# Where TensorE's operand tiles begin in SBUF: 32 bytes past a multiple of 64, or on it

## The chip, the cores and the metric

The kernel runs on one core of a Trainium2 chip. The metric is the device time of one execution in microseconds; of the kernel before there are three runs. A profiled execution of its own gives the trace, whose times count from the first instruction.

## The reference

One layer of a two-branch attention trunk is computed in fp32, for a prompt of 1024 tokens and for 64 sample tokens that carry a cache of 512 keys. The model width is 1024.

```python
h = rms_norm(x, w) @ w_in                       # 1024 -> 6144 columns
sb_q, sb_k, sb_v, sb_z, cb_q, cb_k, cb_v, cb_z, g_sb, g_cb = split(h)
# branch A, stick-breaking: 8 heads x 64
z = q . k * 0.125
log_keep = where(causal, log_sigmoid(-z), 0)
w = where(causal, exp(log_sigmoid(z) + suffix_sum(log_keep)), 0);  o_sb = w @ v
# branch B, chunk band: 8 heads x 64, softmax over at most 576 keys, relative bias
o_cb = softmax(qn . kn * 0.125 + bias) @ v
b_sb = (o_sb * silu(sb_z)) @ w_proj_sb;  b_cb = (o_cb * silu(cb_z)) @ w_proj_cb
y = x + (sigmoid(g_sb) * b_sb + sigmoid(g_cb) * b_cb) @ w_out
```

The new keys and values of both branches are outputs as well.

## The kernel before

T is 1088 columns: 1024 prompt tokens and 64 sample tokens. Every large product is made of three matmuls in the type fp32r. Each operand is split into a high part (a copy rounded to fp32r, on ScalarE) and a low part (the remainder, on GpSimd or VectorE), and high x high, low x high and high x low are summed in PSUM. So each matmul of these products has its own weight load of 128 columns (LDWEIGHTS, "PEld" in the profile), and then streams 256 to 512 columns of the other operand, the moving one. Only the transposes (`ident` is the moving operand) and the product with the values (L1115) are plain fp32.

The program is written out in one order for each engine; no scheduler moves anything. Its stages, as TensorE goes through them:

- **L464**, the projection to values and to the keys and queries of branch B, tokens on the output's partitions: 8 blocks of 256 columns of `w_in`, 9 groups of tokens each. The moving operand is the weights (`whi`, `wlo`, `whix`, `wlox`, 256 columns), the stationary one the normed tokens `xa`, `xm`, `xb` (or `xs` for the sample tokens). That is 8 x (16 + 8 x 24) = 1664 matmuls. Between groups stand transposes at L277, L349 and L371.
- **L634**, the projection to branch A's keys and queries and to the silu gates, by a Strassen-like scheme of seven products: 8 x 7 x 2 x 12 = 1344 matmuls, half of 256 and half of 288 columns. The tokens (`xa`, `xm`, `xb` and their sums `t0h` to `t3l`) move, the weights are stationary.
- **Attention** of both branches, 8 pairs of heads, while L773 fills TensorE with the gates' projections (16 units x 72 = 1152 matmuls, two thirds of 384 and one third of 320 columns). L1024 and L1025 are q.k (224 matmuls each, together 153,600 columns); L1076 transposes the attention weights, L1115 multiplies with the values. Branch A has on VectorE a scan along the keys (L1044) in the tile `kp`, which has three buffers used in turn. L873 (288 matmuls, as wide as L773's) is branch A's projection.
- **L917**, branch B's projection: 192 matmuls of 384 and 96 of 320 columns.
- **L1409** and L1445, the output projection, again by seven products: 672 and 64 matmuls of 256 columns.

The tiles lie in pools. The pools on the left are stacked upwards from `consts`, the pools on the right downwards from the end of SBUF; `xpool` is the first on the right, and holds `xa`, `xm` and `xb`. A tile's address follows from what was opened before it, so a `pad`, a tile that nothing uses, moves all that is stacked behind it:

```python
consts = ctx.enter_context(tc.tile_pool(name="consts", bufs=1))
def pad(pool, n):
    pool.tile([128, n // 4], F32, name=f"pad{n}", bufs=1)
pad(consts, 96)
ident = consts.tile([128, 128], F32, name="ident")
make_identity(nc, ident)
pad(consts, 64)
wpool = ctx.enter_context(tc.tile_pool(name="wp", bufs=2))
...
xpool = ctx.enter_context(tc.tile_pool(name="xn", bufs=1, side="right"))
```

Other pads of 64 bytes stand at the heads of the pools `tp`, `ak`, `am` and `hp`. With all of them, in each matmul but 112 transposes one operand begins 32 bytes and the other 96 bytes past a multiple of 128; in those 112 both begin 96 past. So every operand of TensorE, all 7128 matmuls over, begins 32 bytes past a multiple of 64. Rows inside the tiles keep this, since their lengths and the steps between slices are multiples of 64 bytes.

Of the kernel before, what the change touches and what calls it, by code (L numbers as in the profile page):

```python
# [32 lines left out]
def hybrid_step_kernel(ctx: ExitStack, tc: tile.TileContext, x_prompt, x_sample, c_sbk, c_sbv, c_cbk, c_cbv,  # L33
# [54 lines left out]
    consts = ctx.enter_context(tc.tile_pool(name="consts", bufs=1))  # L88

    def pad(pool, n):  # L90
        pool.tile([128, n // 4], F32, name=f"pad{n}", bufs=1)

    pad(consts, 96)
    ident = consts.tile([128, 128], F32, name="ident")
    make_identity(nc, ident)
    pad(consts, 64)
# [38 lines left out]
    xpool = ctx.enter_context(tc.tile_pool(name="xn", bufs=1, side="right"))  # L135
    x0 = xpool.tile([128, 4, T], F32R, name="xa")
    xm = xpool.tile([128, 2, 4, T], F32R, name="xm")
    x3 = xpool.tile([128, 4, T], F32R, name="xb")
    xhl = [[x0[:], xm[:, 0]], [xm[:, 1], x3[:]]]

    def xk(s, k):
# [1353 lines left out]
```

## Time and profile before

| | |
|---|---|
| median of 3 runs | 1000.83 us (999.85 to 1001.19) |
| profiled execution, span | 1000.1 us, 20177 instructions |
| TensorE: matmul / weight load | 977.8 us (98%) / 930.8 us (93%), 7512 each |
| VectorE / ScalarE / GpSimd | 657.0 us (66%) / 472.9 us (47%) / 324.9 us (32%) |
| granted TensorE clock, mean | 0.998 |
| DMA | 169.83 MB, mean 170 GB/s |

How to read it: the busy time of a matmul counts its way through the array, so that neighbours overlap; what one costs in a stream is the distance from its start to the next one's start. The chain of work gives that distance at once: a row such as "2.73 PE acc L464 x24" is 24 matmuls in 2.73 us with no wait between them. L1115's matmuls stand as two records each, which is why the profile has 7512 and the program 7128.

### The profile page before, as it was taken

To read this page: it belongs to the slowest core of one execution; us is meant where nothing else is said; L and a number is where in the kernel's file an instruction comes from. 1 tells how busy PE (TensorE), PEld (TensorE's weight loads), DVE (VectorE), ACT (ScalarE), POOL (GpSimd) and SP (SyncE) were. 2 spreads that over 40 slices of the span, in tenths; PEclk is the share of its full clock that TensorE was granted. 3 is DMA by queue.
4 is the path that set the end of the run, shared out by engine and by line. 5 is a ranking of instruction groups with operands and counts; after the bars stand their busy time and mean duration, and the time that the engine had idled before them with its cause. 6 is when DMAs were issued, how large, how long until landed. Compare 5 with 4: busy or idle time off the path is not lost.

```text
span 1000.1 us, 20177 instructions
## 1 busy us (share of the span) xinstructions
PE 977.8 (98%) x7512; PEld 930.8 (93%) x7512; DVE 657.0 (66%) x1233; ACT 472.9 (47%) x1075; POOL 324.9 (32%) x338
## 2 busy tenths in 40 slices
PE   5999999999999999999999999999999899999998
PEld 5999999999999999988898888898989798999998
DVE  5456674895455454099898878565766766499735
ACT  5534443444344433277676656454445434365320
POOL 3276663215445543211111101110202200386552
PEclk9999999999999999999999999999999999999999
DMA  7726577424656332786566544765656854773642
GB/s 237 224 92 221 189 249 256 150 91 150 198 155 192 102 97 85 188 228 187 146 166 159 160 114 117 206 200 152 193 150 186 253 168 147 242 224 101 196 136 89
DMA packets 180865, 169.83 MB, mean 170 GB/s; under 512 B 34912, under 2 KB 167136, under 8 KB 180640
## 3 DMA queue, kind: packets, MB, share of 16 engines
q1 hardware_dynamic: 172048, 160.23, 54.2%
q10 hardware_dynamic: 8720, 8.33, 2.6%
q8 instruction: 59, 0.97, 0.4%
q14 instruction: 38, 0.31, 0.1%
HBM read 109.78 MB, written 58.72 MB: 168 GB/s over the span
## 4 chain that ended last, share of the span: by engine, by line
PE 92%; DMA 2%; DVE 2%; ACT 1%; SPq 1%; issue 1%; POOL 1%; DVEq 0%; ACTq 0%
PE acc L464 19%; PE acc L773 18%; PE b L634 17%; PE b L1409 8%; PE o L1115 7%; PE pt L1076 6%; PE b L917 5%; PE z L1025 3%; PE z L1024 3%; PE acc L873 3%; PE pk L349 1%; DMA wrawx<-in_w_in_dram 1%; DMA gt<-d_gsb 1%; DVE be L1045 1%; PE pt L277 1%
## 5 line engine op out<-in xcount | busy, mean ns | idle before, releaser
L122 POOL TENSOR_TENSOR wlo<-wraw,whi 128x1024 fp32r<-128x1024 f32 x30 | 74.2, 2473 | 243.9 <-ACT whi L115 209.2
L773 PE MATMUL acc<-xm,whi 128*128 128x384 f32 (+1 forms) x384 | 128.5, 335 | 0.0
L1044 DVE TENSOR_TENSOR_SCAN kp<-kp,imp 64x576 f32<-64x576 f32 (+8 forms) x72 | 102.8, 1427 | 21.3 <-ACT kp L1027 21.1
L1034 ACT ACTIVATE be<-be,sm 128x640 f32<-128x640 f32 (+5 forms) x72 | 50.8, 705 | 97.1 <-DVE sm L1030 97.1
L1076 PE MATMUL pt<-ident,be 128*128 128x128 f32 (+2 forms) x608 | 90.1, 272 | 6.4 <-DVE wT L1087 3.4
L1085 ACT ACTIVATE wT<-pt 128x512 f32<-128x512 f32 (+3 forms) x130 | 63.6, 502 | 55.1 <-PE pt L1076 55.1
L1076 PEld LDWEIGHTS pt<-ident,be 128*128 128x128 f32 (+2 forms) x608 | 68.5, 140 | 18.4 <-issue 6.4
L464 PE MATMUL acc<-whi,xa 128*128 128x256 f32 x256 | 74.2, 292 | 0.0
L773 PEld LDWEIGHTS acc<-xm,whi 128*128 128x128 f32 x384 | 72.5, 189 | 1.1
L464 PE MATMUL acc<-wlox,xm 128*128 128x256 f32 x256 | 70.8, 278 | 0.0
L464 PE MATMUL acc<-whi,xm 128*128 128x256 f32 x256 | 70.8, 278 | 0.0
L464 PE MATMUL acc<-wlo,xa 128*128 128x256 f32 x256 | 70.7, 278 | 0.0
L464 PE MATMUL acc<-whix,xb 128*128 128x256 f32 x256 | 70.7, 278 | 0.0
L464 PE MATMUL acc<-whix,xm 128*128 128x256 f32 x256 | 70.6, 278 | 0.0
L1115 PE MATMUL o<-wT,vp 128*64 128x256 f32 (+1 forms) x608 | 66.7, 359 | 0.0
L1045 DVE TENSOR_TENSOR be<-be,kp 64x576 f32<-64x576 f32 (+8 forms) x72 | 60.3, 837 | 9.6
L1027 ACT ACTIVATE kp<-z 128x384 f32<-128x384 f32 (+6 forms) x112 | 54.3, 485 | 24.4 <-PE z L1025 22.9
L773 PE MATMUL acc<-xa,wlo 128*128 128x384 f32 (+1 forms) x192 | 65.4, 341 | 0.0
L773 PE MATMUL acc<-xa,whi 128*128 128x384 f32 (+1 forms) x192 | 65.3, 340 | 0.0
L773 PE MATMUL acc<-xm,wlo 128*128 128x384 f32 (+1 forms) x192 | 65.1, 339 | 0.0
L1115 PEld LDWEIGHTS o<-wT,vp 128*64 128x64 f32 x608 | 42.5, 137 | 23.7 <-issue 7.6
L773 PE MATMUL acc<-xb,whi 128*128 128x384 f32 (+1 forms) x192 | 64.0, 333 | 0.0
(298 smaller groups left out, 3017.2 us busy)
## 6 DMA issues: line engine op xcount, KB each, us to landing
wraw<-in_w_in_dram SPq DMA_DIRECT2D x35, 512.0 KB, 4.7
wrawx<-in_w_in_dram SPq DMA_DIRECT2D x13, 512.0 KB, 4.4
sq<-d_qsbT SPq DMA_DIRECT2D x32, 192.0 KB, 4.7
sq<-d_qcbT SPq DMA_DIRECT2D x32, 192.0 KB, 3.7
gt<-d_gsb SPq DMA_DIRECT2D x30, 192.0 KB, 2.7
xt<-in_x_prompt_dram SPq DMA_DIRECT2D x8, 512.0 KB, 5.1
d_kcbT<-hl SPq DMA_DIRECT2D x8, 512.0 KB, 4.5
d_qcbT<-hl SPq DMA_DIRECT2D x8, 512.0 KB, 5.6
```

The costliest lines, as they stand in the source:

```text
L122: (eng or G).tensor_tensor(out=l, in0=raw, in1=h[:].bitcast(F32), op=OP.subtract)
L464: TE.matmul(ps, x, w, start=m == 0, stop=m == len(steps) - 1)
L634: TE.matmul(ps[:, :m], w[:, hl_, k], right[s](x)[:, k, a:b], start=s < 3 and k == 0 and e == 0, stop=k == 3 and e == 2, skip_group_check=s ...
L773: TE.matmul(ps[:, :b - a], w[:, k], xk(x, k)[:, a:b], start=k == 0 and n == 0, stop=k == KT - 1 and n == 2)
L1027: A.activation(kp[:r, x:y], z[:r, :m], AF.Sigmoid, scale=-0.125)
L1034: A.activation(be[:r, :n], be[:r, :n], AF.Exp, bias=kp[:r, j:j + 1], scale=-1.0, accum_out=kp[:r, 2:3])
L1044: V.tensor_tensor_scan(kp[:r, n - 1::-1], kp[:r, n - 1::-1], im[:, ::-1], 0.0, op0=OP.mult, op1=OP.add)
L1045: V.tensor_tensor(out=be[:r, :n], in0=be[:r, :n], in1=kp[:r, 1:n + 1], op=OP.mult)
L1076: TE.transpose(pt[:kr, x, :r], be[:r, kb * 128:kb * 128 + kr], ident[:r, :r])
L1085: A.activation(w[:, sl:sl + m, q0:q0 + r], pt[:, :m, :r], AF.Copy)
L1115: TE.matmul(o[hd * 64:hd * 64 + 64, c0:c1], vv[:kr, kb, hd * 64:hd * 64 + 64], wT[b, p, j, hd, s // 4][:kr, s % 4, c0:c1], start=si == 0, ...
L1409: TE.matmul(ps[:, t], left[s](xs_, k)[:, ts_], wt_[:, k], start=s < 3 and t == k == e == 0, stop=k == 3 and e == 2, skip_group_check=s > 2 ...
```

## The change

One pad grows by 32 bytes, and `xpool` gets a pad of 96 bytes at its tail, which lies below it on the right:

```diff
-    pad(consts, 96)
+    pad(consts, 128)
     ident = consts.tile([128, 128], F32, name="ident")
...
     x3 = xpool.tile([128, 4, T], F32R, name="xb")
+    pad(xpool, 96)
     xhl = [[x0[:], xm[:, 0]], [xm[:, 1], x3[:]]]
```

All tiles on the left move up by 32 bytes, all on the right down by 96. In the built program:

| tile | first byte before (past a multiple of 128) | after |
|---|---|---|
| `ident` | 1248 (96) | 1280 (0) |
| `whi`, first buffer | 10016 (32) | 10048 (64) |
| `xa` | 159712 (96) | 159616 (0) |
| `xs` | 151520 (96) | 151424 (0) |
| `t0h` | 46944 (96) | 46976 (0) |
| `ks`, first buffer | 31072 (96) | 31104 (0) |
| `sq0` | 69536 (32) | 69568 (64) |
| `be`, first buffer | 89504 (32) | 89536 (64) |
| `og0` | 112480 (96) | 112512 (0) |
| `kp`, its three buffers | 124512 (96), 128640 (0), 132768 (32) | 124544 (0), 128672 (32), 132800 (64) |

Modulo 128 everything moves by the same 32 bytes, so that the two operands of a matmul stay 64 bytes apart; modulo 256 the tiles on the right move by 128 bytes against those on the left. Instructions, their order on each engine, their semaphores and their shapes are the same in both programs; nothing but addresses differs. Line numbers behind the added line grow by one.

## The prediction

> **What bounds the kernel now.** I read the page first, then the table of what TensorE waited for, then the chain of waits for the distance between matmuls.
>
> ```profile
> span 1000.1 us, 20177 instructions
> PE 977.8 (98%) x7512; PEld 930.8 (93%) x7512; DVE 657.0 (66%) x1233; ACT 472.9 (47%) x1075; POOL 324.9 (32%) x338
> PEclk9999999999999999999999999999999999999999
> PE 92%; DMA 2%; DVE 2%; ACT 1%; SPq 1%; issue 1%; POOL 1%; DVEq 0%; ACTq 0%
> ```
>
> ```profile
> PE pt L277 <- DVE xn L266: 8.1, 2, 7.4
> PE pt L1076 <- DVE wT L1087: 3.4, 3, 2.4
> PE pt L1076 <- ACT wT L1085: 2.4, 3, 1.3
> PE acc L464 <- ACT whi L115: 2.1, 1, 2.1
> ...
> ```
>
> TensorE is busy for 98% of the span at full granted clock, it makes up 92% of the chain that ended last, and it waited 8.1 us for its first input and a few microseconds altogether after that. The kernel is a stream of matmuls; its time is their number times the distance from one to the next. So a change that alters nothing but addresses matters through that distance, or hardly at all. Here it is, in pieces of the chain without a wait in them (start, length, line, count):
>
> ```profile
> 21.00 0.87 PE pt L277 x8
> 121.04 2.73 PE acc L464 x24
> 124.42 2.84 PE acc L464 x24
> 256.11 30.02 PE b L634 x240
> 865.45 47.37 PE b L917 x288
> 925.53 16.32 PE b L1409 x144
> ```
>
> L464 with 256 columns: 2.73 / 24 = 113.8 ns in one group and 2.84 / 24 = 118.3 ns in the next, with the same code and shapes. L1409, also 256 columns: 16.32 / 144 = 113.3 ns, always. L634, half 256 and half 288 columns (272 on average): 125.1 ns. L917, two thirds 384 and one third 320 (362.7): 164.5 ns. Per column these are 0.443 ns (L1409), 0.460 (L634) and 0.454 (L917). The cost goes with the columns, and it has two levels.
>
> The transposes give the row beside it: a plain fp32 matmul of 128 columns takes 0.87 / 8 = 108.75 ns. If fp32 takes two beats for a column where fp32r takes one (the reading under which a beat, 0.425 ns, comes near the fp32r rates), 256 fp32r columns should cost 108.75 ns too. They cost 113.3 at best. That is 4% more in the quickest stream of the kernel, and 8 to 9% more in the slower ones. For the widest stream, three starts in a row in the timeline:
>
> ```profile
> 700.06 0.40 PE L1024 MATMUL z<-ks,sq 128*128 128x512 f32 x1
> 700.29 0.40 PE L1025 MATMUL z<-ks,sq 128*128 128x512 f32 x1
> 700.53 0.33 PE L773 MATMUL acc<-xm,whi 128*128 128x384 f32 x1
> ```
>
> 235 ns for 512 columns, 0.459 each: twice 113.3 and a little. An excess that doubles with the columns is not a price per instruction; something is paid again and again along the moving operand. Each operand begins 32 bytes past a multiple of 64. If TensorE fetches 64 bytes (16 fp32 columns) at a time, counted from the operand's start, every second fetch straddles a multiple of 128. That is the reason for my forecast. No row shows a straddle, because all operands of before lie alike.
>
> **The change part by part.** Nothing is removed, added or reordered, and no wait changes. Three kinds of access move.
>
> *VectorE, ScalarE, GpSimd.* Before has a natural trial: `kp`'s three buffers take turns, and of each pair of scans below the first uses the buffer that begins on a multiple of 64, the second one that begins 32 past it.
>
> ```profile
> 430.12 0.68 DVE L1044 TENSOR_TENSOR_SCAN kp<-kp,imp 128x256 f32<-128x256 f32 x1
> 431.41 0.68 DVE L1044 TENSOR_TENSOR_SCAN kp<-kp,imp 128x256 f32<-128x256 f32 x1
> 442.99 1.48 DVE L1044 TENSOR_TENSOR_SCAN kp<-kp,imp 128x640 f32<-128x640 f32 x1
> 445.34 1.48 DVE L1044 TENSOR_TENSOR_SCAN kp<-kp,imp 128x640 f32<-128x640 f32 x1
> ```
>
> No difference: 0. The rows of ScalarE and GpSimd hold no such pair; I take 0 for them as well, and TensorE's work covers them: were each 1% slower, that would be 4.7 and 3.2 us spread over the whole span, beside a busy TensorE.
>
> *DMA.* The SBUF ends of all transfers move by 32 or 96 bytes. They are on the path at the start, where this transfer ends last, and a few times later (2% of the chain):
>
> ```profile
> 2.95 7.94 DMA wrawx<-in_w_in_dram
> ```
>
> A tenth of it either way would be 0.8 us; I take 0.
>
> *TensorE.* The sum, at 0.425 ns a column as the clean price, from the transposes:
>
> - L464: between 113.8 and 118.3 I take 116.0; clean 256 x 0.425 = 108.8; 7.2 ns x 1664 = 12.0 us.
> - L634: 125.1 against 115.6; 9.5 x 1344 = 12.8 us.
> - L917 and L873: 164.5 against 154.1; 10.4 x 576 = 6.0 us.
> - L773, the same widths: 10.4 x 1152 = 12.0 us.
> - L1024 and L1025: 153,600 columns x 0.0285 (L917's excess per column) = 4.4 us.
> - L1409 and L1445: 113.3 against 108.8; 4.5 x 736 = 3.3 us.
> - Transposes, L1115: 0. They already run at the clean price.
>
> 50.5 us in all. Bounds for the unknown: above, all of it; below nothing, if every stream fell to the slow level of L464, 118.3 / 256 = 0.462 ns a column. The streams hold 1.76 million columns, which cost today 193 (L464) + 168 (L634) + 284 (L773, L873, L917) + 83 (L1409, L1445) + 70 (L1024, L1025) = 798 us; at 0.462 they would cost 813, so 15 us more.
>
> The Trainium skill (TensorE: Matmul & The Clock Gate, Back-to-back issue gap) gives for a stream of bf16 matmuls at full clock the columns over 2.4 GHz plus about 2.5 ns. That would be 109.2 ns for 256 columns, where this trace has 113.3 to 118.3 in fp32r; by that rule all the excess can go, and the sum would be an estimate of 50 us as well.
>
> What of it reaches the end: L464, L634, L873, L917, L1409 and L1445 are 34.1 us in stages where the chain is TensorE's nearly without a break. In attention, 16.4 us, the others are closer:
>
> ```profile
> 390.00:640.00 250.00, 246.03 (x1749) 221.81 (x1747) 187.31 (x228) 152.99 (x368) 35.46 (x88) 0.99 0.62 163
> 640.00:850.00 210.00, 206.22 (x1499) 186.61 (x1500) 138.74 (x442) 97.32 (x234) 29.88 (x27) 1.00 0.64 181
> ```
>
> ```profile
> 619.76 2.21 DVE kp L1044
> 622.09 1.24 DVE be L1045
> 627.90 3.11 DMA d_gcb<-sg
> 631.58 0.95 ACT whi L115
> ```
>
> VectorE (the third busy time) is at 187 of 250 us there, and around 620 us the chain already leaves TensorE for it. What is late next when TensorE quickens is the long scans; I let two thirds of the 16.4 through, 11. So 34 + 11 = 45 us. The profiled execution spans 1000.1 us and the median is 1000.8; from the latter, 1000.8 - 45 = 955.8, and I say 956.
>
> **The rivals.**
>
> *Only the slow level goes.* The step per column, 0.443 in L1409, may be the port's own rate for 4-byte columns, and only what is above it a matter of where the weight load and the moving operand meet. For: L1409 stands at 113.3 throughout, as if it could not go lower, and begins 32 past a multiple of 64 as L464 does, which jumps between 113.8 and 118.3; so the two levels do not come from the alignment alone. Then 1.76 million columns at 0.443 are 779 us, 19 less, of which 17 come through by the same shares: 984.
>
> *The change does nothing to time.* If the hardware's unit is 32 bytes or smaller, both programs are alike: all operands move by the same 32 bytes modulo 128. For: the scans' rows. Against: VectorE reads a scan of 640 elements in 1.48 us, 2.3 ns an element, a fifth of the rate of TensorE's stream; so what it hides, TensorE need not. 1000.8. The Trainium skill (SBUF — State Buffer, Specifications) speaks of 16-byte cachelines; 32 is a multiple of 16, and by that rule nothing moves. No run here shows a line's size.
>
> *Slower: the streams lock.* The next weight load reads SBUF while the present matmul streams. Today each fetch lies across two 64-byte halves; on a multiple of 64 it lies in one, and two readers that meet in the same half wait for each other every time instead of by half. The two levels of L464 show that some meeting of this kind exists and that it stays for a whole group of 24. Besides, tiles on the right move by 128 bytes modulo 256 against those on the left, which can swap quick groups for slow ones. Place: L464, L634, L773, L917, L1409. Price: all at 0.462, +15 us, 1016, since a slower TensorE is on the path everywhere. It decides once L1409 and more than half of L464's groups stand at 118.
>
> **How the numbers follow.** The straddle goes: 0.36, 956. Only the slow level goes: 0.2, 984. Nothing: 0.17, 1000.8. Slower: 0.27, 1016 and less. The step that goes with the columns speaks for the first, and that VectorE sees nothing against it; for a mere shift by 32 bytes I see fewer ways to lose than to gain. The range reaches from the whole 50.5 us and the rounding of the rows (0.01 us in 24 matmuls, 2.5 us over all 5,920 fp32r matmuls), 948, to 1016; the first case alone would be 948 to 966. About 0.2% is what a measurement of this kernel can tell from no change. Faster by more than that: 0.56; within it: 0.17; slower: 0.27.
>
> **What would show it.** Right: L1409's pieces of 144 at 15.7 us or less instead of 16.32, L917's 288 at about 44.4, L464 without two levels, transposes unchanged at 0.87 for 8, scans unchanged, and a chain in attention with more of VectorE in it. The second case: L1409 still 16.32, L464 all at 2.73. Wrong altogether: L1409 at 16.32 and L464 as mixed as now, or L1409 at 17.

## The result

The change made no difference that these runs can tell: 1001.53 us (median of 13 runs, 999.27 to 1004.06) against 1000.76 us before (median of 13, 998.66 to 1001.86), a ratio of 1.0008 with a 95% interval of 0.9999 to 1.0016. Of the four cases it is "the change does nothing to time", which had 0.17; the forecast was 956 us.

The page of the changed kernel has TensorE where it was (its busy time was 977.8 us), and the scans whose buffers changed places among themselves (before: 102.8 us, 1427 ns each):

```profile
span 1000.5 us, 20177 instructions
PE 978.2 (98%) x7512; PEld 930.2 (93%) x7512; DVE 659.3 (66%) x1233; ACT 472.8 (47%) x1075; POOL 327.0 (33%) x338
PE 87%; DVE 4%; DMA 4%; ACT 2%; issue 1%; SPq 1%; POOL 1%; DVEq 0%; ACTq 0%; POOLq 0%
L1045 DVE TENSOR_TENSOR_SCAN kp<-kp,imp 64x576 f32<-64x576 f32 (+8 forms) x72 | 102.8, 1428 | 21.2 <-ACT kp L1028 21.0
```

The last ended chain leaves TensorE more often than before (PE 92%, DVE 2%), which the prediction had named as a sign of a quicker TensorE; here it came without any gain, so it is no such sign.

The same pieces of the chain as before (start, length, line, count; lines are one higher):

```profile
20.59 0.87 PE pt L278 x8
120.31 2.83 PE acc L465 x24
123.79 2.73 PE acc L465 x24
256.16 29.89 PE b L635 x240
925.92 16.32 PE b L1410 x144
```

The output projection takes 16.32 us for 144, to the hundredth what it took. L635's 240 take 29.89 instead of 30.02. In the input projection the two levels are both there still, and something has changed after all: the group that took 2.73 us before (at 121.04) now takes 2.83, and the one behind it, 2.84 before (at 124.42), takes 2.73. Over all 72 groups of that line, by the distance of starts in the two traces, 35 were at the quick level before and 31 are now, in different places: 24 groups became slow and 20 quick. (The first of the 72 waits for its inputs in every trace and counts as slow.)

### The profile page after: what moved, and what is told of

Its sections match the earlier page's. It is cut to its first block, busy times and chain, and to the rows that moved or that the text cites. A ratio compares the mean times of both kernels' runs of the same rounds, so it can differ in the third digit from the quotient of the medians.

```text
span 1000.5 us, 20177 instructions
## 1 busy us (share of the span) xinstructions
PE 978.2 (98%) x7512; PEld 930.2 (93%) x7512; DVE 659.3 (66%) x1233; ACT 472.8 (47%) x1075; POOL 327.0 (33%) x338
## 4 chain that ended last, share of the span: by engine, by line
PE 87%; DVE 4%; DMA 4%; ACT 2%; issue 1%; SPq 1%; POOL 1%; DVEq 0%; ACTq 0%; POOLq 0%
PE acc L465 19%; PE b L635 17%; PE acc L774 16%; PE b L1410 8%; PE o L1116 6%; PE pt L1077 6%; PE b L918 4%; PE z L1026 3%; PE z L1025 3%; PE acc L874 2%; DMA ot<-d_osb 1%; DVE be L1046 1%; PE pk L350 1%; DMA gt<-d_gsb 1%; DVE kp L1045 1%
## 5 line engine op out<-in xcount | busy, mean ns | idle before, releaser
L1045 DVE TENSOR_TENSOR_SCAN kp<-kp,imp 64x576 f32<-64x576 f32 (+8 forms) x72 | 102.8, 1428 | 21.2 <-ACT kp L1028 21.0
```

What stands on the lines that cost most here:

```text
L1045: V.tensor_tensor_scan(kp[:r, n - 1::-1], kp[:r, n - 1::-1], im[:, ::-1], 0.0, op0=OP.mult, op1=OP.add)
```

## The experiments

Two kinds: kernels with matmuls added behind the last one of before, where other engines have nearly stopped (one profiled execution each, their whole times not compared), and pads changed in the kernel itself (5 to 12 runs each, beside runs of before, whose medians were 1000.1 to 1000.4 us).

**Starts and distances, measured alone.** `tk0` is sliced for the moving operand (`M`), `tk1` for the stationary one (`S`), at so many bytes past a multiple of 128 (128 past one of 256 in both tiles); the first pair is 0 and 64.

```diff
+    R = range(96)
+    for _ in R: TE.matmul(pr[:, 0:256], S(64), M(0, 256), start=True, stop=True)     # L1473
+    for _ in R: TE.matmul(pr[:, 0:256], S(96), M(32, 256), start=True, stop=True)    # L1474
+    ... # M,S: 0,0  32,32  0,32  0,96  32,0  32,64  0,192  0,128  4,64  16,64  0,68  0,80
+    for _ in R: TE.matmul(pr[:, 0:128], S(64), M(0, 128), start=True, stop=True)     # L1487
+    ... # 192, 288, 320, 384, 512 columns
```

> The kernel before with 20 groups of 96 fp32r matmuls added behind its last one, when the other engines have nearly stopped. The operands are cut from the tiles tk0 and tk1 at chosen bytes modulo 128; groups 1 to 14 move 256 columns, groups 15 to 20 move 128, 192, 288, 320, 384 and 512. Theory A, own rate: TensorE takes 4-byte columns at 17/16 of the plain price wherever they begin, and the second level is the next weight load meeting the stream. Then no group of 256 goes below 113 ns, starts at 4 or 16 bytes past included; 512 columns take 227 ns or more; groups differ by the distance between the two operands (modulo 64 or 128), with 113 or 118 ns, not by where both lie. Theory B, fetches smaller than I assumed: 64 bytes is the wrong unit, 16 or 32 is the right one; then a start at 4 bytes past (group 11) is slower than group 1 by several per cent, and all starts on multiples of 32 are alike. Theory C, other engines cause the excess: all groups of 256 fall to about 109 ns, since nothing else runs.

The chain runs through the added groups one after the other (the view begins inside the first):

```profile
996.92 7.49 PE acc L1473 x66
1004.41 11.30 PE acc L1474 x96
1015.71 11.50 PE acc L1475 x96
1027.21 11.51 PE acc L1476 x96
1038.72 11.36 PE acc L1477 x96
...
1106.74 11.52 PE acc L1483 x96
...
1152.46 10.67 PE acc L1487 x96
1163.12 10.75 PE acc L1488 x96
...
1200.78 16.77 PE acc L1491 x96
1217.55 22.40 PE acc L1492 x96
```

In ns for one matmul of 256 columns: 113.5 at 0 and 64, 117.7 at 32 and 96, 119.8 and 119.9 where both begin at the same byte (0 and 0, 32 and 32), 118.3 at 0 and 32. A start 4 bytes past (L1483) costs 120.0, no more than two equal starts on a multiple of 64. No group falls to 109: theory C is out, the other engines have no part in the excess. 384 columns take 174.7 and 512 take 233.3, with the operands on multiples of 64. So what I took for a straddle is paid by operands that begin on multiples of 64. Theory B is met by half: the start at 4 bytes is slower than the first group, but starts on multiples of 32 are not alike (113.5 to 119.9). Theory A stands so far, with one puzzle: 0 and 64, 32 and 96 have the same distance and differ by 4 ns, as a theory of place would have it.

**What goes with the columns.**

```diff
+    for _ in R: TE.matmul(pr[0:128, 0:512], S(64, 128), M(0, 512), start=True, stop=True)  # L1475
+    for _ in R: TE.matmul(pr[0:64, 0:512], S(64, 64), M(0, 512), start=True, stop=True)    # L1476
+    for _ in R: TE.matmul(pr[0:32, 0:512], S(64, 32), M(0, 512), start=True, stop=True)    # L1477
+    ... # plain fp32 with 128 and 256 columns: L1481, L1482
+    ... # bf16 with 128, 256, 384, 512 columns: L1483 to L1486
```

> The kernel before with groups of 96 matmuls added behind its last one: fp32r with a stationary operand of 128, 64 and 32 columns and 512 moving ones, then 384 x 64, 256 x 64, 256 x 32; plain fp32 with 128 and 256 moving columns; bf16 with 128, 256, 384 and 512 moving columns. Theory A, own rate of 4-byte columns: fp32r stays at 0.443 ns a column whatever the stationary width (227 ns for 512, 113 for 256), and bf16 goes below it (about 109 ns for 256 and 215 for 512). Theory D, the weight load makes the whole excess: with 64 and 32 stationary columns the excess over 0.425 ns a column shrinks to a half and a quarter, so that 512 columns come to about 220 ns; bf16, whose weight load is shorter, gains as well.

This view, too, begins inside the first group:

```profile
996.96 20.30 PE acc L1475 x87
1017.26 22.33 PE acc L1476 x96
1039.59 22.24 PE acc L1477 x96
...
1078.48 11.42 PE acc L1479 x96
1089.91 11.20 PE acc L1480 x96
1101.11 21.44 PE acc L1481 x192
1122.55 41.44 PE acc L1482 x192
1163.99 5.36 PE acc L1483 x96
1169.35 10.48 PE acc L1484 x96
1179.83 15.60 PE acc L1485 x96
```

With 128, 64 and 32 stationary columns, 512 moving columns take 233.3, 232.6 and 231.7 ns: a weight load of a quarter of the size takes off 1.6 ns, so theory D fails. 256 columns with 64 and 32 stationary ones (L1479, L1480) take 119.0 and 116.7 ns, more than the 113.5 with 128. Theory A's figure of 227 ns for 512 is missed as well; no single price per column fits.

bf16 takes 55.8, 109.2 and 162.5 ns for 128, 256 and 384 columns, what the formula of the Trainium skill (TensorE: Matmul & The Clock Gate, Back-to-back issue gap) gives. The same section names about 81 ns for 128 columns in a stream of weight loads and matmuls; these groups are such a stream, and here the measured 55.8 decides. For 384 columns fp32r took 174.7 in the run above. The bf16 operands begin at the same byte modulo 256, which costs fp32r 120 ns instead of 113.5. Plain fp32 leaves two records for a matmul, each of 215.8 ns for 256 columns, which is just under twice the 109.2 ns of bf16: no excess there either, if a column takes two beats in each record. So the excess, 4 to 10% over bf16 at 256 columns and 7.5% at 384, shows in fp32r alone, whose 4-byte columns come at about one a beat.

Why they cannot be taken faster no run was made to show, but a stretch in the trace of the run mod256 below narrows it. There the granted clock was 0.50 for some microseconds, and six matmuls of 320 columns in fp32r (L874, which is L873 of before) stood in a row (first the row of the stretch: its length, TensorE's busy time, clock, the DMA engines' share and GB/s; then the piece of the chain):

```profile
795.20:797.00 1.80, 1.80 (x8) 0.50 1.00 244
795.61 1.60 PE acc L874 x6
```

That is 266.7 ns for one, 0.833 ns a column, to the rounding of the row twice the 0.4167 ns that a further column costs bf16 at full clock (55.8 to 162.5 ns over 256 columns). At full clock 320 columns took 146.7 ns (14.08 us for 96, L1490 of the first of these kernels), 0.458 a column. So at half the clock fp32r has no excess: it is no fixed number of extra beats, but time that a slower clock hides. What needs that time stays open.

**Half the change, the left.**

```diff
-    pad(consts, 96)
+    pad(consts, 128)
```

> Only the first half of the change (the first pad of consts 96 to 128, no pad in xpool): the tiles on the left move by 32 bytes, xa, xm and xb stay. In L464, L773, L873, part of L634 and a part of L1409 the two operands then stand 32 bytes apart modulo 64 instead of 0, and only one of them begins on a multiple of 64. Theory A with a meeting of the two reads: those lines change their share of slow groups, so the time moves by 3 us or more, most likely up (1005 to 1015); L917 stays at 47.4 us for 288. If neither the distance nor the place matters: 1000.8, same as before.

Slower, by less than 1% but clear of no change: 1008.43 us, ratio 1.0079 (1.0065 to 1.0093). **The right half** is the other line of the change, `pad(xpool, 96)`, alone:

> Only the second half of the change (the pad of 96 bytes in xpool, consts as before): xa, xm, xb and the other tiles on the right move by 96 bytes down, the left stays. The operands of L464, L773, L873 and of parts of L634 and L1409 then stand 32 bytes off a distance of 64, with the aligned one being the other than in the run of the left half. If the distance alone counts: as in the run of the left half, 1006 to 1010, with L464 slower by about 5 us. If what counts is that the moving operand of L464 lies on a multiple of 64: 1001 or less.

Slower too, at the lower edge of what I expected: 1005.99 us, ratio 1.0060 (1.0046 to 1.0074). **Both operands at the same byte**, for the lines that read `xa`, `xm` and `xb`:

```diff
     make_identity(nc, ident)
-    pad(consts, 64)
+    pad(consts, 128)
```

> The second pad of consts is 128 instead of 64, so that in L464, L773, L873, in the parts of L634 and L1409 that read xa, xm and xb, and in the transposes of L1076 both operands begin at the same byte modulo 128, instead of 64 apart. Theory A with a meeting of the two reads in units of 64 or 128 bytes: these lines go to the slow level or beyond, 0.462 ns a column or more, at least 8 us in all: 1009 to 1030; transposes of L1076 above 109 ns. If the distance does not matter either: 1000.8 and the mix of 113 and 118 as now.

1007.76 us, ratio 1.0081 (1.0066 to 1.0095). I had put 1009 as its lower end, and the transposes at L1076, whose operands begin at the same byte now, did not suffer (109 ns as before). The chain of the three runs at the same places, the left half first, then the right half, then the same byte:

```profile
119.66 2.83 PE acc L464 x24
870.60 47.62 PE b L917 x288
918.22 11.23 PE b L1409 x96
```

```profile
118.20 2.81 PE acc L465 x24
867.67 47.35 PE b L918 x288
915.02 11.23 PE b L1410 x96
```

```profile
119.81 2.88 PE acc L464 x24
917.78 11.16 PE b L1409 x96
930.76 16.32 PE b L1409 x144
```

L464 has lost its quick groups in all three (none stands below 116.4 ns); the piece of L1409 with the groups that read `xa` and `xb` takes 11.16 to 11.23 us for 96 instead of 10.91; L917 (47.62 and 47.35 against 47.37) and the parts of L1409 whose two operands moved together (16.32) are as before. By the distance of starts, L464 takes 5.4, 2.5 and 5.1 us more in the three traces, where I had expected about 5 for the right half too; L1409 takes 1.0 to 1.3 more and L634 0.4 to 1.0. So each half of the change costs 6 to 8 us by altering the distance between two operands, and the whole, which restores it modulo 128, costs nothing. In the right half L464's moving operand is as it was and its stationary one lies on a multiple of 64; in the left half it is the other way round. Neither helps.

**What ran before.** Back to the puzzle: groups of 24 behind 2, 3, 4 and 5 plain fp32 matmuls, at the same starts each time.

```diff
+    for k in range(96): TE.matmul(*mm(S(64, k), M(0, k)), **K)      # L1475; L1476 at 32, 96; both again
+    for r in range(4):
+        for k in range(2 + r): TE.matmul(*F(S(0, k)), **K)          # L1480, plain fp32, two records each
+        for k in range(24): TE.matmul(*mm(S(64, k), M(0, k)), **K)  # L1481, M at 0, S at 64
+    ... # the same at 32,96 (L1484)  0,192 (L1487)  32,224 (L1490)  0,0 (L1493)  32,32 (L1496)
```

> The kernel before with groups of fp32r matmuls of 256 columns added behind its last one, on slices of tk0 and tk1 that advance as a product's do. First four groups of 96 in turn with the moving and the stationary operand at 0 and 64, 32 and 96, 0 and 64, 32 and 96 bytes past a multiple of 256. Then six sets of four groups of 24, each group behind 2 to 5 plain fp32 matmuls of 128 columns: at 0 and 64, 32 and 96, 0 and 192, 32 and 224, 0 and 0, 32 and 32. Theory A1, history: the level (113.3 or 117.8 ns) of two operands 64 apart is set by how the weight load and the stream stood to each other when the group began; then groups of the same addresses show both levels, and 0/64 is not the quick one throughout. Theory A2, place: a start on a multiple of 64 is quick and one 32 past it is slow; then all groups at 0/64 are at 113.3 and all at 32/96 at 117.8, and the result of the change is only hidden by something else. Both: 0/0 and 32/32 at 120.

```profile
993.70 10.89 PE acc L1475 x96
1004.59 11.31 PE acc L1476 x96
1015.89 10.91 PE acc L1477 x96
1026.81 11.31 PE acc L1478 x96
...
1038.56 2.83 PE acc L1481 x24
1041.39 0.67 PE acc L1480 x6
1042.06 2.83 PE acc L1481 x24
1044.89 0.89 PE acc L1480 x8
1045.78 2.74 PE acc L1481 x24
...
1052.91 2.83 PE acc L1484 x24
1055.74 0.67 PE acc L1483 x6
1056.41 2.75 PE acc L1484 x24
```

The four groups of 96 repeat the puzzle: 0 and 64 quick, 32 and 96 slow, both times. But each stands behind the other kind, so they cannot tell place from what went before; the groups of 24 can. At 0 and 64 the third of four groups is quick (2.74 us), the others are slow; at 32 and 96 the first is slow and three are quick. Both starts show both levels, so the place does not set them (A2 fails), and what went before does (A1); by which way, no run shows. Where both operands began at the same byte, all eight groups took 2.86 to 2.88. I had not expected the last part: at a distance of 192 instead of 64 (0 and 192, 32 and 224) one group in eight was quick, 2.73, and seven took 2.83.

**Distances modulo 256.** The change moves the tiles on the right by 128 bytes modulo 256 against the left. That part alone:

```diff
     x3 = xpool.tile([128, 4, T], F32R, name="xb")
+    pad(xpool, 128)
```

> The kernel before with a pad of 128 bytes in xpool: no operand changes its place modulo 128, but the tiles on the right move by 128 bytes against the left modulo 256, as they do in the change too. If distances count modulo 128 only: 1000.8, within 2 us. If they count modulo 256: L464 and L634 change their mix of levels, by 2 to 5 us either way, and the change's result was this part and the alignment in balance.

1000.55 us, ratio 1.0003 (0.9994 to 1.0012): the time does not move by the 2 to 5 us that I expected if distances modulo 256 counted, though the levels below do change places. **And the shift alone**, all operands on multiples of 64 and all distances kept, modulo 256 too:

```diff
-    pad(consts, 96)
     ident = consts.tile([128, 128], F32, name="ident")
...
     x3 = xpool.tile([128, 4, T], F32R, name="xb")
+    pad(xpool, 96)
```

> The kernel before without the first pad of consts and with the pad of 96 bytes in xpool, so that every tile on both sides moves down by 96 bytes: all operands of TensorE begin on multiples of 64, and no distance between two of them changes, not even modulo 256. In the trace of the change the groups of L464 stand at 113 and 118 ns in exactly the places of the run with the pad of 128 bytes in xpool, and in other places than before. If only distances count: this kernel has before's pattern, group for group (the group of 24 near 121 us in 2.73 us, the one near 124 us in 2.84), L1409 with 144 in 16.32, and 1000.4 within 1.5 us. If the place counts as well, and the distance modulo 256 hid it in the change: L464, L634 or L773 differ from before by 2 us or more.

1000.53 us, ratio 1.0005 (0.9994 to 1.0016). The chain of the run with 128 bytes first, then that of the pure shift:

```profile
120.47 2.83 PE acc L465 x24
123.95 2.73 PE acc L465 x24
924.75 16.32 PE b L1410 x144
```

```profile
120.61 2.73 PE acc L464 x24
124.00 2.84 PE acc L464 x24
923.70 16.32 PE b L1409 x144
```

The first pair is the changed kernel's (2.83, 2.73), the second pair before's (2.73, 2.84). It holds for all 72 groups of the line, by the distance of starts in the four traces: the pure shift has before's levels in 72 of 72, and the run with 128 bytes has the changed kernel's in 72 of 72. So the change splits cleanly. Its alignment to 64 bytes altered no level in L464; in L634, 3 of 112 stretches of 12 matmuls differ between before and the pure shift by more than 1 ns a matmul, 0.2 us in all. Its movement modulo 256 took the quick level from some groups of L464 and gave it to others, 31 instead of 35, 4 groups of 0.1 us or 0.4 us, which is less than these runs resolve.

## Why the prediction was wrong, point by point

- **What bounds the kernel**: right. TensorE's stream, and the distance between matmuls as the only way in. The halves of the change moved that distance by some ns and the time by 6 to 8 us.
- **The straddle**: this step failed. The forecast rests on the excess coming from where operands begin, so that a start on a multiple of 64 takes it away, 50.5 us. With every operand on a multiple of 64 and every distance kept, the kernel took 1000.53 us, and L1409's 144 took 16.32 us as before. The excess is there wherever the operands begin.
- **The clean price** of 0.425 ns a column, from the transposes: this failed with it. It is what a beat costs in bf16 and in plain fp32, but no group of fp32r at full clock reached it: 113.3 ns for 256 at best and 231.7 to 233.3 for 512 on multiples of 64. The sum of 50.5 us was counted against a rate that no run shows for this type. The reading behind it, two beats for a column of plain fp32, fits the transposes alone: a plain fp32 matmul of 128 columns left two records of 111.7 ns each (L1481), twice the 108.75 ns of a transpose and a little.
- **"An excess that doubles with the columns is not a price per instruction"**: the excess does go with the columns, and I drew too much from it. It shows that the stream itself is slower; it does not show that the cause lies in where the stream begins. I said that no row shows a straddle because all operands lie alike. With no row for it, "does nothing" deserved a chance nearer to the forecast's.
- **VectorE, ScalarE, GpSimd, DMA at 0**: nothing contradicts it. Of the pairs of scans in the prediction it is the second, not the first, that uses the buffer on a multiple of 64; their times are equal, so the reading stands. All the scans took 102.8 us though two of their three buffers now begin on a multiple of 64 instead of one; VectorE's 659.3 and GpSimd's 327.0 us are within 2.3 us of before.
- **"Only the slow level goes"** (984): its ground was right, 113.3 is the lowest that any group of 256 reached at full clock; that alignment would bring all groups there was not. The levels come from distance and from what ran before.
- **"The streams lock"** (1016): how the two operands lie to each other does have a price, which shows at equal starts (120 ns) and in three kernels at 1.0060 to 1.0081; that it is two reads which meet is argued, not shown. But it goes with the distance, and the change keeps that modulo 128. I had written down that both operands move together and did not use it here: a mechanism between two tiles cannot see a shift of both. Its side remark, that the movement by 128 bytes modulo 256 can change which groups are quick, came true, with 0.4 us and not 15.
- **"Does nothing"**: came true, for the reason given, that all moves alike modulo 128. The pure shift shows it apart from the rest. The Trainium skill's 16-byte cachelines (SBUF — State Buffer, Specifications) fit that; starts of 4 and 16 bytes past were run only together with other distances, so whether the unit is 16 or 32 bytes stays open.

## What to carry to other kernels

Ask first what a change of addresses keeps: if all tiles move alike, only a mechanism that knows absolute places can respond, and here none did to a shift from 32 past a multiple of 64 onto it. What counts for two operands of one matmul is the distance between their starts: 64 bytes apart modulo 128 was the best of those tried, and the only one with groups at 113; a distance of 0 or 32 cost up to 6% of a 256-column matmul and 0.6 to 0.8% of this kernel. And take the clean price of a stream from its own element type, not from another one.

## What the runs showed of the hardware that I had not expected

- At full clock fp32r is slower than bf16 at the same widths (174.7 against 162.5 ns for 384 columns), with a stationary operand of 32 columns as of 128 (231.7 and 233.3 ns for 512). At half the clock it keeps pace: 0.833 ns a column, twice bf16's 0.4167 at full clock.
- With 128 and with 192 moving columns a matmul of this type took 111 to 112 ns (L1487, L1488), as did each record of plain fp32 with 128 (111.7), while bf16 with 128 took 55.8: at these widths something else than the stream sets the pace. I take it for the weight load, which no run here separates.
- A group that has settled keeps its level, 113.4 or 117.8 ns, to its end, and in L464 the levels come back exactly in another build whose distances are the same: 72 groups of 72. By the traces before and after, a stationary operand 64 bytes ahead of the moving one modulo 256 was quick in 22 and 21 groups of 32, one 192 ahead in 11 and 6 of 32 (L464, the groups of prompt tokens).
